# Seven block products for three of the eight branch-gate groups in a hybrid decoder trunk

## The chip, the core and the metric

One NeuronCore of one Trainium2 chip runs the whole trunk. The metric is device time in microseconds (us), the median of several runs. TensorE (PE) has matmuls and weight loads, VectorE (DVE) and ScalarE (ACT) do elementwise work, GpSimd (POOL) issues the accumulating DMAs and SyncE (SP) the other DMAs.

## The reference

Two layers on x (512 tokens, 1024 channels), all in float32. In each layer

- h = RMSNorm(x), and h @ w_in gives all mixers' inputs and the gates, 4 x 1024 columns;
- four branches y_i, 512 wide: sparse attention (A), a convolution module with a 31-tap convolution, a LayerNorm and a swish (B), a short gated convolution (C), stick-breaking attention (D);
- merged = sum over i of sigmoid(gate_i(h) + b_gate_i) * (y_i @ w_o_i), and x = x + merged @ w_merge;
- x = x + FFN(RMSNorm(x)), with gate and up products of 2816 columns, a 3-tap convolution on the gate, and a down product.

## The kernel before, in words

Float32 operands go through the array as float32r pairs: `split` (L187, L188) writes hi = a rounded copy (ACT) and lo = source - hi (DVE), and each product is three matmuls, hi*hi, hi*lo and lo*hi, by `mm` (L123). Activations lie with channels on partitions and 512 tokens on the free side. The normed x is `xh`, `xl`, eight tiles of 128 channels.

Weights come in **units** of 512 KB (1024 elements a partition). `plan` lists all units in the order of use; `ahead` (called by `weights` at each unit) keeps three units split, so that the one in use has two behind it, by `split_weights` (hi on ACT at L414, lo on DVE at L415, three buffers of each). `channels` multiplies one call's units: a unit of 256 columns is two column halves c with 12 matmuls each of 512 tokens, and between the halves it calls `amid`. Outputs take two of four PSUM banks `mm`; other work has four banks `at`.

`amid` calls `tick(budget)`, which emits side jobs from three queues against a budget in us; a job that has several stages gets one stage a tick. `need(labels)` emits, at one place, all that is left up to the labels. PE and DVE run their instructions in the order in which the program emits them (`manual_schedule`, L1349, L707); ACT, POOL and SP are ordered by the scheduler while the mixing runs. In the FFN (L1148) ACT is in emitted order too, and `amid` emits what the dictionary `beside` holds for the running unit number (`slot`).

`merge(n, y)` (L1004 on) takes the branches in the order C, A, D, B (n = 0 to 3). For each of four pairs jj it multiplies 256 gate columns (two units, 1024 inputs), takes the sigmoid on ACT (L1013), multiplies 256 columns of the branch's output map w_o (one unit, 512 inputs), and on DVE multiplies by the gate (L1025) and adds to `merged` (L1027; for n = 3, L1029 and a split).

In queue 2 stand the 31 taps of branch B (L893), then `ln_sum`, a pause, `ln_center` (one product with a constant, then DVE and ACT in turn, L916 to L922), a pause, `ln_root` (four one-column products, a square root on ACT at L278, a reciprocal on DVE at L281), `spread` (four transposes on PE at L286, a copy at L288) and the job `ln`: four `ln_out(c)`, each a DVE multiply (L933), a Silu (L934) and a `split`. They are emitted by the ticks of n = 2 with budget B_M2; after n = 2 stands `need("ln")`, and n = 3 runs with budget 0.

The FFN's gate and up products are done already as **seven block products** (Strassen-Winograd): for 256 + 256 columns, tokens in two halves of H = 256 and inputs in two halves of 512, seven products of a 512 x 256 block with a 512 x 256 block in place of eight. `product` issues 24 matmuls of 256 tokens for each. Their weight blocks are sums, made by accumulating DMAs from GpSimd (`load_sum`, `grow`, L393): s = u1 + u2, then + g1 after the product s1, and so on. The operands are `comb`: "b11", "n1", "b21", "b22" in `xh`, `xl` (written by `feed_ffn`, which keeps first half and difference for the first four tiles), and "t3", "n2", "t4" in tiles of `pieces()`, made by `feed_sums` (two scaled copies on ACT at L251, three DVE operations at L253 to L255, two splits). Partial outputs f, v, y, z pass between products by copies and adds (`start_y` L1172, `keep_y` L1176, `start_z` L1187, `up_half` L1190).

Of the kernel before, what the change touches and what calls it, by code (L numbers as in the profile page):

```python
# [27 lines left out]
P = 128  # L31
# [46 lines left out]
def trunk(ctx: ExitStack, tc, x, positions, g_mix, w_in, b_gate, g_qa, g_ka, g_kidx, w_oa,  # L78
# [15 lines left out]
    def s_tile(w=516, dtype=F32):  # L94
        return tmp.tile([P, w], dtype, tag="s", name=nm("s"), bufs=10)
# [14 lines left out]
    def q4_tile():  # L110
        return act.tile([P, 2, T], F32R, tag="q4", name=nm("q4"), bufs=8)
# [46 lines left out]
    def col(name, i):  # L158
        c = place[name] + i
        return par[:, c:c + 1]  # L160
# [63 lines left out]
    def feed_ffn(k, l):  # L224


        g = col("g_ffn", l * KD + k)
        if k == 0:
            pieces()
# [13 lines left out]
        for i, name in enumerate(("b11", "n1") if k < 4 else ("b21", "b22")):  # L243
            comb[name, k % 4] = [a[k][:, i * H:(i + 1) * H] for a in (xh, xl)]
        squared(k)

    def feed_sums(j, l):

        e1, e2, d, d4 = s_tile(), s_tile(), s_tile(), s_tile()
        for e, k in ((e2, j + 4), (e1, j)):  # L250
            nc.scalar.activation(e[:, :T], xT[k], AF.Copy, scale=col("g_ffn", l * KD + k))  # L251
        t3, n2, t4 = d[:, :H], d[:, H:T], d4[:, :H]
# [9 lines left out]
        comb["t4", j] = four  # L262

    def inv_root(acc, n, rows, sums=None, banks=None):

# [41 lines left out]
    def ffn_block(w, l, h, f):  # L307
        return w[l, h * 512:(h + 1) * 512, f * P:(f + 2) * P]
# [12 lines left out]
    def ffn_order():  # L321
# [4 lines left out]
        for n in range(1, last + 1):  # L326
# [11 lines left out]
            else:  # L338
                yield from ((n, "s3"), (m, "g1"), (n, "s4"), (n, "u2"), (m, "s2"), (m, "g2"))

    def plan():
        for l in range(L):
            for c0, w, nk in V_CHUNKS:
                yield from in_units(l, O_AV + c0, w, nk)
            for p in range(2):
                yield from in_units(l, O_GLU + 512 + 256 * p, 256)
                yield from in_units(l, O_GLU + 256 * p, 256)
            for c in range(2):
                yield from in_units(l, O_AQ + 512 * c, 512, 2)
            for p in range(2):  # L350
                for n in (1, 2, 0):
                    yield from in_units(l, O_CC + 512 * n + 256 * p, 256)
            for n, (branch, w_o) in enumerate(MERGES):
                if n == 1:
                    for i in range(4):
                        yield from in_units(l, O_SB + 256 * i, 256)
                    yield from in_units(l, O_SB + 1024, 512, 2)
                for jj in range(4):
                    yield from in_units(l, O_GATE + branch * D + jj * 256, 256)
                    yield w_o[l, :, jj * 256:(jj + 1) * 256], 0, 4, 256  # L360
            for p in range(4):
# [25 lines left out]
    GROWS = {"s1": ("s", "g1"), "g1": ("g1", "u1"), "s2": ("s", "g2")}  # L387

    def part_of(l, n, name):
        return ffn_block(w_ffn_gate if name[0] == "g" else w_ffn_up, l, int(name[1]) - 1, 2 * n)  # L390

    def grow(l, n, to, what):
# [144 lines left out]
    def tokens(units, ops, w, after=None, between=None, banks=None):  # L537
# [5 lines left out]
        for n, (src, k0, nk, _) in enumerate(units):  # L543
# [15 lines left out]
            if between:  # L559
                tick(budget[0])  # L560
        return ps

    xop = list(zip(xh, xl))

# [110 lines left out]
    def mixing(l, first):  # L675
# [323 lines left out]
                split(y[:, 0], y[:, 1], cv[c][:, :T])  # L999
                yc.append(y)  # L1000

        merged = [None] * KD

        def merge(n, y):  # L1004

            branch, w_o = MERGES[n]
            yop = [(a[:, 0], a[:, 1]) for a in y]
            for jj in range(4):
# [8 lines left out]
                if n == 3:  # L1017
                    hi = q4_tile()
                for c in range(2):
                    j = jj * 2 + c  # L1020
                    if n == 0:
                        merged[j] = mf_tile()
                        nc.vector.tensor_tensor(merged[j], g[c], gs[c][:, :T], op=OP.mult)
                        continue
                    nc.vector.tensor_tensor(gs[c][:, :T], g[c], gs[c][:, :T], op=OP.mult)  # L1025
                    if n < 3:
                        nc.vector.tensor_tensor(merged[j], merged[j], gs[c][:, :T], op=OP.add)  # L1027
                        continue
                    nc.vector.tensor_tensor(gs[c][:, :T], merged[j], gs[c][:, :T], op=OP.add)  # L1029
                    lo = act.tile([P, T], F32R, tag="mf", name=nm("mlo"), bufs=8)  # L1030
                    split(hi[:, c], lo, gs[c][:, :T])
                    merged[j] = (hi[:, c], lo)

        budget[0] = B_M0
        merge(0, yc)
# [92 lines left out]
    BLOCK_OF = {"g1": "b11", "s1": "n1", "s2": "n2", "g2": "b21", "s3": "t3", "s4": "b22",  # L1128
                "u2": "t4"}

    def product(l, n, step, bank):

        hi, lo = block_weights(l, n, step)
        for c in range(2):
            dst = bank[:, c * H:(c + 1) * H]
            for k in range(4):
                oh, ol = comb[BLOCK_OF[step], k]
                w = slice(c * P, (c + 1) * P)
                mm(dst, hi[:, k, w], oh, start=step in ("g1", "s1") and c == k == 0, stop=False)
                mm(dst, hi[:, k, w], ol, start=False, stop=False)  # L1140
                mm(dst, lo[:, k, w], oh, start=False, stop=k == 3)
            if c == 0:
                amid()

    def ffn(l, last):
        done.clear()
        order.close()
        order.enter_context(tc.manual_schedule(engines={E.PE, E.DVE, E.Activation}))  # L1148
# [301 lines left out]
```

## Time and profile before

| what | before |
|---|---|
| median of three runs | 1959.0 us (1958.98 to 1959.74) |
| the profiled execution: time, span | 1959.04 us, 1957.3 us |
| PE busy | 1944.5 us, 99% |
| PE weight loads busy | 1681.5 us, 86% |
| DVE busy | 1407.7 us, 72% |
| ACT busy | 926.5 us, 47% |
| DMA | 237.84 MB, mean 122 GB/s |

The two layers take the same course, 967.3 us apart. A row of the chain gives start, length, the engine with what it did, and a count: "PE mm" are matmuls into the banks `mm`, "PE at" into the banks `at`. A row of a timeline gives start, length, engine, line, operation, output<-input and shape, and in brackets the idle time of the engine before it and what ended that. Where matmuls follow one another, each one's length contains its passage through the array; the distance of starts is the length of a whole row divided by its count.

### The profile page before, as it was taken

To read this page: it belongs to the slowest core of one execution; us is meant where nothing else is said; L and a number is where in the kernel's file an instruction comes from. 1 tells how busy PE (TensorE), PEld (TensorE's weight loads), DVE (VectorE), ACT (ScalarE), POOL (GpSimd) and SP (SyncE) were. 2 spreads that over 40 slices of the span, in tenths; PEclk is the share of its full clock that TensorE was granted. 3 is DMA by queue.
4 is the path that set the end of the run, shared out by engine and by line. 5 is a ranking of instruction groups with operands and counts; after the bars stand their busy time and mean duration, and the time that the engine had idled before them with its cause. 6 is when DMAs were issued, how large, how long until landed. Compare 5 with 4: busy or idle time off the path is not lost.

```text
span 1957.3 us, 27555 instructions
## 1 busy us (share of the span) xinstructions
PE 1944.5 (99%) x10691; PEld 1681.5 (86%) x10691; DVE 1407.7 (72%) x2462; ACT 926.5 (47%) x1494; POOL 120.9 (6%) x173
## 2 busy tenths in 40 slices
PE   9999999999999999999999999999999999999998
PEld 7878888888888998989888888888888889999897
DVE  7887789768446783777867878897674477648675
ACT  6436442443634663634553464424445366546253
POOL 0000000000000210201000000000000012112010
PEclk9999999999999999999999999999999999999999
DMA  6333233323532995966343332332345349769562
GB/s 200 106 97 86 68 89 97 96 98 108 150 97 75 194 202 117 202 166 114 122 129 97 86 87 76 87 97 86 105 122 137 96 98 201 183 134 219 128 120 87
DMA packets 219513, 237.84 MB, mean 122 GB/s; under 512 B 7638, under 2 KB 206838, under 8 KB 218358
## 3 DMA queue, kind: packets, MB, share of 16 engines
q1 hardware_dynamic: 172918, 189.93, 31.7%
q0 software_dynamic: 46464, 46.14, 15.7%
q8 instruction: 84, 1.38, 0.3%
q14 instruction: 47, 0.39, 0.1%
HBM read 229.75 MB, written 6.29 MB: 121 GB/s over the span
## 4 chain that ended last, share of the span: by engine, by line
PE 95%; ACT 2%; DVE 1%; DMA 1%; issue 1%; ACTq 0%; SPq 0%; DVEq 0%; POOLq 0%
PE mm L123 79%; PE at L123 14%; DMA b<-in_w_ffn_gate_dram 1%; ACT hi L414 1%; PE at L841 0%; PE at L1085 0%; PE at L806 0%; DVE lo L415 0%; ACT s L251 0%; PE at L1376 0%; DMA x<-in_x_dram 0%; DVE s L1327 0%; PE at L286 0%; ACT L1214 0%; PE at L745 0%
## 5 line engine op out<-in xcount | busy, mean ns | idle before, releaser
L414 ACT ACTIVATE hi<-raw 128x1024 fp32r<-128x1024 f32 (+2 forms) x297 | 310.4, 1048 | 508.2 <-PE mm L123 460.8
L415 DVE TENSOR_TENSOR lo<-raw,hi 128x1024 fp32r<-128x1024 f32 (+3 forms) x295 | 357.6, 1215 | 207.5 <-ACT hi L414 207.0
L123 PE MATMUL mm<-xh,hi 128*128 128x512 f32 (+1 forms) x1184 | 445.2, 376 | 0.0
L123 PE MATMUL mm<-xh,lo 128*128 128x512 f32 (+1 forms) x1184 | 437.5, 369 | 0.0
L123 PE MATMUL mm<-xl,hi 128*128 128x512 f32 (+1 forms) x1184 | 437.1, 369 | 0.0
L123 PE MATMUL mm<-q,hi 128*128 128x512 f32 x1200 | 381.7, 391 | 0.0
L123 PEld LDWEIGHTS mm<-q,hi 128*128 128x128 f32 x1200 | 224.2, 188 | 47.8 <-issue 2.1
L123 PE MATMUL mm<-q,lo 128*128 128x512 f32 x664 | 258.5, 389 | 0.0
L123 PEld LDWEIGHTS mm<-xh,hi 128*128 128x128 f32 x1184 | 223.3, 189 | 40.6 <-issue 2.8
L123 PEld LDWEIGHTS mm<-xl,hi 128*128 128x128 f32 x1184 | 223.4, 189 | 38.0 <-issue 1.0
L123 PEld LDWEIGHTS mm<-xh,lo 128*128 128x128 f32 x1184 | 223.2, 189 | 38.3
L893 DVE SCALAR_TENSOR_TENSOR b<-b,par,b 128x512 f32<-128x512 f32 x240 | 180.3, 751 | 6.9
L123 PEld LDWEIGHTS mm<-q,lo 128*128 128x128 f32 x664 | 124.6, 188 | 26.0
L123 PE MATMUL at<-xh,lo 128*128 128x256 f32 x480 | 135.8, 283 | 0.0
L123 PE MATMUL at<-xl,hi 128*128 128x256 f32 x480 | 135.8, 283 | 0.0
L123 PE MATMUL at<-xh,hi 128*128 128x256 f32 x480 | 135.8, 283 | 0.0
L123 PE MATMUL mm<-m,hi 128*128 128x256 f32 x660 | 127.0, 283 | 0.5 <-DVE m L188 0.5
L415 DVE TENSOR_TENSOR lo<-b,hi 128x1024 fp32r<-128x1024 f32 x66 | 80.8, 1224 | 61.2 <-ACT hi L414 61.2
L123 PE MATMUL mm<-hi,xh 128*128 128x512 f32 (+1 forms) x320 | 120.3, 382 | 0.6 <-ACT hi L414 0.3
L123 PE MATMUL mm<-lo,xh 128*128 128x512 f32 (+1 forms) x320 | 117.9, 374 | 0.0
L123 PE MATMUL mm<-hi,xl 128*128 128x512 f32 (+1 forms) x320 | 117.8, 374 | 0.0
L414 ACT ACTIVATE hi<-b 128x1024 fp32r<-128x1024 f32 x66 | 69.9, 1059 | 94.6 <-PE mm L123 38.0
(271 smaller groups left out, 3023.5 us busy)
## 6 DMA issues: line engine op xcount, KB each, us to landing
raw<-in_w_in_dram SPq DMA_DIRECT2D x152, 512.0 KB, 3.6
b<-in_w_ffn_gate_dram POOLq DMA_DIRECT2D x44, 512.0 KB, 6.6
raw<-in_w_ffn_down_dram SPq DMA_DIRECT2D x43, 512.0 KB, 4.4
gu<-in_w_ffn_gate_dram SPq DMA_DIRECT2D x22, 512.0 KB, 4.7
b<-in_w_ffn_up_dram SPq DMA_DIRECT2D x22, 512.0 KB, 5.3
b<-in_w_ffn_up_dram POOLq DMA_DIRECT2D x22, 512.0 KB, 6.0
raw<-in_w_ffn_gate_dram SPq DMA_DIRECT2D x22, 512.0 KB
raw<-in_w_ffn_up_dram SPq DMA_DIRECT2D x22, 512.0 KB, 3.7
```

Source lines behind the costliest of these rows:

```text
L123: return nc.tensor.matmul(*a, skip_group_check=True, **k)
L414: nc.scalar.activation(hi[:, k:k + step], raw[:, k:k + step], AF.Copy)
L415: nc.vector.tensor_tensor(lo, raw, hi.bitcast(F32), op=OP.subtract)
L893: nc.vector.scalar_tensor_tensor(a[:, :T], u[c][:, j:j + T], col(f"cb_w{l}", j * 4 + c), a[:, :T], op0=OP.mult, op1=OP.add)
```

## The change

For n = 2 (branch D) the pairs jj = 2, 3 and for n = 3 (branch B) all four pairs are no longer multiplied plainly (`plain_pairs`). Each two pairs, 512 gate columns, are a group done by `gates(n, half, yop)`: seven `product` calls, with the two w_o units of the group at places 0 and 3 of nine. Six groups in two layers are changed; the w_o products, sigmoids, multiplies and adds are the same in number of elements. From the first group on ACT is in emitted order too, and `amid` emits from `beside`, no ticks.

The operands for the groups are made of the normed x: `whole(k)` adds xh and xl; four jobs `sums{j}` after `ln` in queue 2 make "t3", "n2", "t4"; `difference(j)` turns the second half of the first four tiles into a difference. They are wanted at n = 2, jj = 1, between the gate product and the w_o product, with `need("ln", sums0 to sums3)` and four `difference`. `pieces()` is called before n = 2 instead of in `feed_ffn`. The FFN makes its own operands as before.

```diff
+    def whole(k):
+        e = s_tile()
+        nc.vector.tensor_tensor(e[:, :T], xh[k].bitcast(F32), xl[k].bitcast(F32), op=OP.add)
+        return e
+
+    def difference(j):
+        e, d = whole(j), s_tile()
+        nc.vector.tensor_tensor(d[:, :H], e[:, :H], e[:, H:T], op=OP.subtract)
+        split(xh[j][:, H:], xl[j][:, H:], d[:, :H])
...
+    GATE_ORDER = (0, "s1", "g1", 1, "s2", "g2", "s3", "s4", "u2")
+    def plain_pairs(n):
+        return (4, 4, 2, 0)[n]
...
-            for jj in range(4):
+            for jj in range(plain_pairs(n)):
                 g = channels(in_units(l, O_GATE + branch * D + jj * 256, 256), xop, 256)
...
+                if n == 2 and jj == 1:
+                    need("ln", *[f"sums{j}" for j in range(4)])
+                    for j in range(4):
+                        difference(j)
                 g = channels([(w_o[l, :, jj * 256:(jj + 1) * 256], 0, 4, 256)], yop, 256)
+                add_branch(n, jj, g, gs)
+            for half in range(plain_pairs(n) // 2, 2):
+                if slot[0] is None:
+                    slot[0] = 0
+                    order.close()
+                    order.enter_context(tc.manual_schedule(engines={E.PE, E.DVE, E.Activation}))
+                gates(n, half, yop)
...
+            def start_y():
+                v["y"] = ps_at()
+                if first_gates[0]:
+                    v["z"] = ps_at()
+                    for name in "yz":
+                        mm(v[name], identb, zero_diag, start=True, stop=True)
+                nc.scalar.activation(v["y"], v["f"], AF.Copy)
...
+            put(3, start_y)
+            put(5, lambda: keep_y("y2"))
+            put(6, start_z, lambda: sigmoids("f", 0, 0, 1.0))
+            put(7, lambda: keep_y("y3"))
+            put(8, up_half, lambda: sigmoids("z", 0, 1, 1.0), lambda: sigmoids("y3", 2, 1, -1.0),
+                lambda: add_branch(n, 2 * half, v[0], gs[:2]))
+            put(9, lambda: sigmoids("y", 2, 0, -1.0),
+                lambda: add_branch(n, 2 * half + 1, v[1], gs[2:]))
+            for step in GATE_ORDER:
+                if isinstance(step, int):
+                    c = (2 * half + step) * 256
+                    v[step] = channels([(w_o[l, :, c:c + 256], 0, 4, 256)], yop, 256)
+                    continue
+                name = {"g1": "f", "g2": "f", "s1": "v", "s4": "z"}.get(step, "y")
+                if step in ("g1", "s1"):
+                    v[name] = ps_at()
+                product(l, (branch, half), step, v[name])
...
         done.add("room")
+        pieces()
+        for j in range(4):
+            job(2, f"sums{j}", ["ln"], (5.4, lambda j=j: sums(j, whole(j), whole(j + 4))))
         budget[0] = B_M2
+        first_gates[0] = True
         merge(2, yd)
-        need("ln")
-        budget[0] = 0.0
         merge(3, yb)
```

## Rows read from the trace of the kernel before

**Rows 1.** The page, part 1 (busy time of the engines) and part 2 (PE in 40 slices)

```profile
PE 1944.5 (99%) x10691; PEld 1681.5 (86%) x10691; DVE 1407.7 (72%) x2462; ACT 926.5 (47%) x1494; POOL 120.9 (6%) x173
...
PE   9999999999999999999999999999999999999998
```

**Rows 2.** Waits of PE, whole span, longest first: us in total, times, longest

```profile
PE at L123 <- DVE s L1190: 1.7, 1, 1.7
PE mm L123 <- ACT s L1176: 1.3, 2, 0.6
```

**Rows 3.** Chain of waits, 400 to 720 us

```profile
440.30 38.09 PE mm L123 x168
478.39 0.86 PE at L123 x2
479.25 10.92 PE mm L123 x48
490.18 0.79 PE at L123 x8
490.96 5.59 PE mm L123 x24
496.56 0.44 PE at L286 x4
...
687.33 5.76 PE at L123 x48
```

**Rows 4.** Timeline of DVE, first layer, n = 2 and the feeding of the FFN

```profile
467.77 0.74 DVE L893 SCALAR_TENSOR_TENSOR b<-b,par,b 128x512 f32<-128x512 f32 x1
...
486.52 1.22 DVE L415 TENSOR_TENSOR lo<-raw,hi 128x1024 fp32r<-128x1024 f32 x1
...
491.30 0.18 DVE L281 RECIPROCAL rt<-rt 128x4 f32<-128x4 f32 x1 [1.66 <-ACT rt L278]
491.39 0.66 DVE L1025 TENSOR_TENSOR s<-mm,s 128x512 f32<-128x512 f32 x1
...
497.66 0.69 DVE L933 TENSOR_TENSOR b<-b,s 128x512 f32<-128x512 f32 x1 [1.23 <-ACT s L288]
501.26 0.69 DVE L188 TENSOR_TENSOR q<-b,q 128x512 fp32r<-128x512 f32 x1 [2.91 <-ACT q L187]
...
518.72 0.68 DVE L933 TENSOR_TENSOR b<-b,s 128x512 f32<-128x512 f32 x1
524.20 0.69 DVE L188 TENSOR_TENSOR q<-b,q 128x512 fp32r<-128x512 f32 x1 [4.79 <-ACT q L187]
...
631.30 0.43 DVE L253 TENSOR_TENSOR s<-s,s 128x256 f32<-128x256 f32 x1 [0.51 <-ACT s L251]
...
633.50 0.42 DVE L188 TENSOR_TENSOR m<-s,m 128x256 fp32r<-128x256 f32 x1
```

**Rows 5.** Timeline of ACT, first layer, n = 2

```profile
487.32 1.06 ACT L414 ACTIVATE hi<-raw 128x1024 fp32r<-128x1024 f32 x1 [0.86 <-ACT s L1013]
488.28 0.67 ACT L1013 ACTIVATE s<-mm,par 128x512 f32<-128x512 f32 x1
488.97 1.28 ACT L278 ACT_TABLE_LOAD   x1
491.00 0.26 ACT L278 ACTIVATE rt<-at,eps 128x4 f32<-128x4 f32 x1 [0.75 <-PE at L123]
...
497.03 0.60 ACT L288 ACTIVATE s<-at 128x512 f32<-128x512 f32 x1 [2.27 <-PE at L286]
...
498.94 0.82 ACT L934 ACTIVATE b<-b,par 128x512 f32<-128x512 f32 x1
...
500.61 0.61 ACT L187 ACTIVATE q<-b 128x512 fp32r<-128x512 f32 x1
```

**Rows 6.** Timeline of PE, the first microseconds

```profile
1.19 3.17 PE L123 MATMUL at<-s 128*128 128x512 bf16 x7 [1.19 <-DVE s L1364]
...
13.77 2.01 PE L123 MATMUL mm<-hi,xl 128*128 128x324 f32 x12
```

**Rows 7.** Engines by stretch; then DMA issues: KB each, us to landing

```profile
640.00:690.00 50.00, 49.13 (x409) 48.72 (x408) 38.17 (x59) 33.73 (x45) 11.69 (x10) 1.00 1.02 206
...
b<-in_w_ffn_gate_dram POOLq DMA_DIRECT2D x44, 512.0 KB, 6.6
```

More of the change, by code (lines that the diff above doesn't have):

```diff
@@ L247, in feed_sums, with sums @@
     def feed_sums(j, l):
-        e1, e2, d, d4 = s_tile(), s_tile(), s_tile(), s_tile()
+        e1, e2 = s_tile(), s_tile()
         for e, k in ((e2, j + 4), (e1, j)):
             nc.scalar.activation(e[:, :T], xT[k], AF.Copy, scale=col("g_ffn", l * KD + k))
+        sums(j, e1, e2)
+    def sums(j, e1, e2):
+        d, d4 = s_tile(), s_tile()
         t3, n2, t4 = d[:, :H], d[:, H:T], d4[:, :H]
@@ L357, in plan @@
                     yield from in_units(l, O_SB + 1024, 512, 2)
-                for jj in range(4):
+                for jj in range(plain_pairs(n)):
                     yield from in_units(l, O_GATE + branch * D + jj * 256, 256)
                     yield w_o[l, :, jj * 256:(jj + 1) * 256], 0, 4, 256
+                for half in range(plain_pairs(n) // 2, 2):
+                    for step in GATE_ORDER:
+                        if isinstance(step, str):
+                            yield l, (branch, half), step
+                        else:
+                            c = (2 * half + step) * 256
+                            yield w_o[l, :, c:c + 256], 0, 4, 256
             for p in range(4):
@@ L561, in tokens, with product @@
         return ps
+    BLOCK_OF = {"g1": "b11", "s1": "n1", "s2": "n2", "g2": "b21", "s3": "t3", "s4": "b22",
+                "u2": "t4"}
+    def product(l, n, step, bank):
+        hi, lo = block_weights(l, n, step)
+        for c in range(2):
+            dst = bank[:, c * H:(c + 1) * H]
+            for k in range(4):
+                oh, ol = comb[BLOCK_OF[step], k]
+                w = slice(c * P, (c + 1) * P)
+                mm(dst, hi[:, k, w], oh, start=step in ("g1", "s1") and c == k == 0, stop=False)
+                mm(dst, hi[:, k, w], ol, start=False, stop=False)
+                mm(dst, lo[:, k, w], oh, start=False, stop=k == 3)
+            if c == 0:
+                amid()
     xop = list(zip(xh, xl))
@@ L1000, in mixing @@
                 yc.append(y)
-        merged = [None] * KD
+        merged, first_gates = [None] * KD, [True]
         def merge(n, y):
@@ L1007, in merge @@
             yop = [(a[:, 0], a[:, 1]) for a in y]
-            for jj in range(4):
+            for jj in range(plain_pairs(n)):
                 g = channels(in_units(l, O_GATE + branch * D + jj * 256, 256), xop, 256)
@@ new lines, in merge, with add_branch @@
+            for half in range(plain_pairs(n) // 2, 2):
+                if slot[0] is None:
[3 more added lines that the diff above has]
+                gates(n, half, yop)
+        def add_branch(n, jj, g, gs):
+            if n == 3:
+                hi = q4_tile()
+            for c in range(2):
+                j = jj * 2 + c
+                if n == 0:
+                    merged[j] = mf_tile()
+                    nc.vector.tensor_tensor(merged[j], g[c], gs[c][:, :T], op=OP.mult)
+                    continue
+                nc.vector.tensor_tensor(gs[c][:, :T], g[c], gs[c][:, :T], op=OP.mult)
+                if n < 3:
+                    nc.vector.tensor_tensor(merged[j], merged[j], gs[c][:, :T], op=OP.add)
+                    continue
+                nc.vector.tensor_tensor(gs[c][:, :T], merged[j], gs[c][:, :T], op=OP.add)
+                lo = act.tile([P, T], F32R, tag="mf", name=nm("mlo"), bufs=8)
+                split(hi[:, c], lo, gs[c][:, :T])
+                merged[j] = (hi[:, c], lo)
@@ new lines, in gates, with put, keep_y, start_z @@
+        def gates(n, half, yop):
+            branch, w_o = MERGES[n]
+            v, i = {}, slot[0]
+            gs = [None] * 4
+            def put(k, *fs):
+                beside.setdefault(i + k, []).extend(fs)
+            def start_y():
[5 more added lines that the diff above has]
+                nc.scalar.activation(v["y"], v["f"], AF.Copy)
+            def keep_y(name):
+                v[name] = s_tile()
+                nc.scalar.activation(v[name][:, :T], v["y"], AF.Copy)
+            def start_z():
+                if not first_gates[0]:
+                    v["z"] = ps_at()
+                first_gates[0] = False
+                nc.vector.tensor_tensor(v["z"], v["v"], v["y2"][:, :T], op=OP.add)
+            def up_half():
+                nc.vector.tensor_tensor(v["y3"][:, :T], v["v"], v["y3"][:, :T], op=OP.add)
+            def sigmoids(src, tiles, h, sign):
+                for c in range(2):
+                    t = tiles + c
+                    if gs[t] is None:
+                        gs[t] = s_tile()
+                    nc.scalar.activation(
+                        gs[t][:, h * H:(h + 1) * H], v[src][:, c * H:(c + 1) * H], AF.Sigmoid,
+                        bias=col("b_gate", l * 32 + branch * 8 + half * 4 + t), scale=sign)
+            put(3, start_y)
[6 more added lines that the diff above has]
+                lambda: add_branch(n, 2 * half + 1, v[1], gs[2:]))
+            for step in GATE_ORDER:
+                if isinstance(step, int):
+                    c = (2 * half + step) * 256
+                    v[step] = channels([(w_o[l, :, c:c + 256], 0, 4, 256)], yop, 256)
+                    continue
+                name = {"g1": "f", "g2": "f", "s1": "v", "s4": "z"}.get(step, "y")
+                if step in ("g1", "s1"):
+                    v[name] = ps_at()
+                product(l, (branch, half), step, v[name])
@@ L1125, in mixing @@
                     feed_sums(2 * p + c - 4, l)
[L1128 to L1143, printed above, removed]
+        assert not beside
+        slot[0] = None
     def ffn(l, last):
         done.clear()
-        order.close()
-        order.enter_context(tc.manual_schedule(engines={E.PE, E.DVE, E.Activation}))
         rows = act.tile([P, T], F32, tag="rows", name=nm("rows"), bufs=1)
```

23 lines of the change are left out of this document (6 added, 17 removed).

## Prediction, made before the change was run

> **What bounds the kernel now.** I read the page first: PE is busy 99% of the span, in every one of 40 slices [rows 1]. Busy alone could hide small waits, so I read PE's waits next: the longest is 1.7 us in one place, the next 1.3 us in two [rows 2]. TensorE is a full queue from end to end. So a matmul taken out gives back its whole distance to the next one, and any new wait of PE costs its whole length: there is no slack to swallow it. The third view, the chain, gives the distances: 168 matmuls of 512 tokens in 38.09 us are 0.2267 us each, 48 of 256 tokens in 5.76 us are 0.1200 us each [rows 3]. Half the tokens cost 53%, not 50%.
>
> **What is removed and added on PE.** A group of 512 gate columns is two pairs of two units: 4 x 24 = 96 matmuls of 512 tokens, 96 x 0.2267 = 21.77 us. As seven products it is 7 x 24 = 168 matmuls of 256 tokens, 168 x 0.1200 = 20.16 us. A group saves 1.61 us, six save 9.6 us, 4.8 a layer. Against it stand two zero products a layer (the first `start_y`): 512 columns each, by the nearest row 0.23 us, so 0.5 us a layer. This is all that the change can win: 1959.0 - 9.6 + 0.9 = 1950.
>
> The Trainium skill ("TensorE: Matmul & The Clock Gate", "Back-to-back issue gap") gives N/2.4 + 2.5 ns between matmuls; by that a group would save 2.4 us and six some 14 us, an estimate from that page. Here the trace disagrees, with 226.7 and 120.0 ns against 215.8 and 109.2, and I keep the rows.
>
> **What is moved: LayerNorm, sums and differences before the first group.** This is the largest term. In n = 2 of the kernel before, DVE's timeline lets each tick be found: the last tap at 467.77, the LayerNorm's mean, the reciprocal of `ln_root` at 491.30, `ln_out(0)` at 497.66, and `ln_out(3)` from 518.72 to 524.89 [rows 4]. Each tick stands at the middle of a unit. The chain shows them from PE's side: the one-column products of `ln_root` at 490.18 [rows 3] are in the middle of the w_o unit of jj = 1. The new `need` stands half a unit earlier, at 490.18 - 12 x 0.2267 = 487.5. At that point the last pause is over, but `ln_root`, `spread`, four `ln_out`, four `sums` and four `difference` are all still to come, with no unit of matmuls between them.
>
> What PE still has: with three units split ahead, the w_o unit of jj = 1 and the first w_o unit of the group, 48 x 0.2267 = 10.9 us. Behind them comes the product s1. It wants "n1", which the `difference` calls make, and the split of its weights, which `ahead` emits after the burst. DVE keeps the emitted order: at 491.30 it stood 1.66 us idle for a root although the split and adds behind it wanted nothing of it [rows 4]. So s1 waits for the whole burst.
>
> The burst, in the first layer's clock. PE does the one-column products until 488.2. The root waits on ACT for its table, which ends at 488.97 + 1.28 = 490.25, then takes 0.26 [rows 5]; with the reciprocal (0.18) `spread` can start at 490.8. PE is in order too and stands 2.6 us. It goes on at 491.3 (0.44 of transposes) and reaches s1 at 491.3 + 10.9 = 502.2. DVE meanwhile:
> - the copy of `spread`, 0.60, until 491.9 [rows 5];
> - `ln_out(0)`: as before 497.66 to 501.95, with a table load, 4.3 us [rows 4], until 496.2;
> - `ln_out(1 to 3)`: multiply 0.69, Silu 0.82, copy 0.61, lo 0.69 one after the other, with hand-overs 2.9 us each [rows 4, 5], until 504.9;
> - four `sums`: `feed_sums` takes 2.62 us of DVE from 631.30 to 633.92 and each `whole` 0.66 more [rows 4], 3.94 us each, until 520.7;
> - four `difference`: 0.66 + 0.43 + a copy of at most 0.61 + 0.42, some 2.0 us each, until 528.7;
> - lo of s1, 1.22 us [rows 4], until 529.9.
>
> PE waits 529.9 - 502.2 = 27.7 us, with `spread` 30.3 us a layer. From below: if no ACT step held DVE, its instructions alone are 8 x 0.69 + 4 x (1.32 + 3 x 0.43 + 0.69 + 0.42) + 4 x 1.51 + 1.22 = 27.6 us from 487.7 on, until 515.3, against PE at 499.6: 16 us. From above: were each `ln_out` as long as the last one before, 6.2 us, it would be 42 us. I take 30, since with the sigmoids of later gates gone there is one Silu table load where before there were four. Behind DVE's burst stand the adds of jj = 1 and the split of g1, 2.7 + 1.2 us after s1's; s1's own matmuls cover most of that.
>
> **The clock after such a wait.** PE's first matmuls take 3.17 / 7 = 0.45 us for 512 columns, twice the 0.2267 of later, so the lower level, 1.2 GHz; at 13.77 twelve of 324 columns take 2.01 us, 0.17 each, the upper one [rows 6]. No long idle stretch lies inside the trace, so what 27 us of idleness do is bounded: nothing, or half of the 12.6 us from 1.19 to 13.77, 6.3 us. PE was starting and stopping in that stretch and would run densely here; I take 2 us a layer. (The same page, "What's actually happening", holds the throttled level to be what an idle array falls back to; no run here shows it yet.)
>
> **Inside the groups.** Between g2 and s3, s4, u2 no other unit stands. `start_z` comes at the middle of s3 on DVE behind a split (1.22) that waits for a hi (1.06): g2's end + 1.06 + 1.22 + 0.69 = 2.97 against s4 at + 2.88: 0.1 to 0.3 us. The unit after u2 wants the banks of the first w_o unit, free after `up_half` and a multiply: 1.06 + 1.22 + 0.69 + 0.69 = 3.7 us after u2's start, against 2.88: 0.8 us. After the layer's last group the second merge unit needs the last two tiles of `merged`, whose sigmoids, multiplies, adds and splits are emitted only at the middle of the first merge unit; by the same durations DVE and ACT end some 4 us late. From above that is 3 x 1.1 + 4 = 7 us a layer; from below nothing, as the FFN hands partial sums on in the same way at a PE without waits [rows 2, 3]. The gates have less between their steps than the FFN, so I take 4. Weights: a group loads ten units' worth in some 31 us; the FFN's start moves more (DMA share 1.02, PE 49.13 of 50 us [rows 7]), so I put nothing for it. `pieces()` earlier only takes free tiles: nothing.
>
> **Sum.** A layer: - 4.8 + 0.5 + 30.3 + 2 + 4 = + 32; two layers + 64. The profiled execution took 1959.04 us, the median is 1959.0, so the sum stands against either: 2023 us.
>
> **Rivals.**
> 1. *Faster: DVE gets there in time.* The place is the lo of s1: if the burst ends by 502.2, the matmul count decides and the time is 1950. For it: DVE is only 72% busy over the span [rows 1]. Against: even DVE's bare instructions end at 515.3. Chance 0.05.
> 2. *The burst is covered, but the hand-overs in the groups are not*: 1950 + 2 x 7 = 1964. It needs the same condition. Chance 0.04.
> 3. *The burst, and weights that come late besides.* After the wait each group goes through accumulating loads of 6.6 us from issue to landing [rows 7], and s2 needs one that starts when s1 is split. Some 5 us for each of six groups on top: 2050. For it: the DMA share near 1 with such blocks [rows 7]; against: PE stayed dense there. Chance 0.09.
> 4. *The forecast*, chance 0.82.
>
> **Range and chances.** With the lower bound of the burst and nothing for clock and groups, it is 1959 + 2 x (- 4.3 + 16) = 1982; with all the upper bounds, 1959 + 2 x (- 4.3 + 42 + 6.3 + 7) = 2061. All ends meeting is unlikely; 1990 to 2046 leaves out rivals 1 and 2 and about half of what lies at the far ends. A difference below 0.2%, 4 us, is what a measurement of this kernel could not tell from none; of the cases only rival 2 comes near it. Faster 0.05, same 0.02, slower 0.93.
>
> **What would show it.** In the changed profile: two idle stretches of PE of 20 to 35 us, one a layer, ended by DVE's lo of a "b" block or its operand, ahead of the first 256-token products of the mixing; in front of them on DVE L933, the new `whole`, `sums`, `difference`, without a matmul unit between. The products' distance should be 0.1200, and 1008 more matmuls of 256 tokens stand for 576 of 512. The forecast is wrong if PE has no wait above 10 us, or if DVE's burst begins before the end of the gate of jj = 1.

## The result and the profile after

The changed kernel takes 2058.7 us (median of five runs, 2057.6 to 2059.8) against 1959.0 us: a ratio of 1.0508, interval 1.0497 to 1.0519. It is slower by 99.7 us, 49.9 us a layer. The forecast was + 32 a layer, 2023 us, and its range ended at 2046: the direction was right and the time lies outside.

The page of the changed kernel, parts 1 and 2, to be laid beside [rows 1]:

```profile
PE 1958.2 (95%) x11127; PEld 1706.0 (83%) x11127; DVE 1477.4 (72%) x2572; ACT 951.8 (46%) x1566; POOL 151.7 (7%) x197
...
PE   9999999997699899999999999999958998999998
...
PEclk9999999999799999999999999999979999999999
```

PE now has two holes, one a layer, at slices 10 and 11 and at 30 and 31, and a shallower one a layer at slices 14 and 34. In the third row the granted clock, at its upper level throughout in the kernel before, falls at slices 11 and 30. Its mean over the span is 0.978 (1.000 before), so with two levels some 45 us of each layer lie at 1.2 GHz (0.022 x 2 x 2055.8 / 2).

Waits of PE in the changed kernel, longest first (us in total, times, longest), beside [rows 2]:

```profile
PE at L124 <- ACT xh L188: 40.4, 2, 20.2
PE at L124 <- DVE lo L451: 13.8, 4, 6.5
PE at L124 <- ACT hi L450: 10.4, 2, 5.2
PE mm L124 <- ACT q L188: 5.3, 4, 1.3
PE at L305 <- DVE rt L300: 5.3, 2, 2.6
PE mm L124 <- DVE s L1092: 3.7, 6, 0.6
```

Every one comes two or more times, as the two layers take the same course. The timeline of PE in the first layer places the first two rows, ahead of the first product and inside it:

```profile
503.56 0.39 PE L124 MATMUL mm<-q,lo 128*128 128x512 f32 x1
524.16 0.58 PE L124 MATMUL at<-xh,hi 128*128 128x256 f32 x1 [20.21 <-ACT xh L188]
524.62 0.58 PE L124 MATMUL at<-xl,hi 128*128 128x256 f32 x1
531.65 0.58 PE L124 MATMUL at<-xh,lo 128*128 128x256 f32 x1 [6.46 <-DVE lo L451]
```

After two matmuls on the first tile of "n1" PE needs the lo of the weights. The timeline of DVE shows why that is last (the burst; compare [rows 4]):

```profile
490.80 0.18 DVE L300 RECIPROCAL rt<-rt 128x4 f32<-128x4 f32 x1 [2.83 <-ACT rt L297]
492.88 0.69 DVE L986 TENSOR_TENSOR b<-b,s 128x512 f32<-128x512 f32 x1 [1.90 <-ACT s L307]
...
506.46 0.69 DVE L189 TENSOR_TENSOR q<-b,q 128x512 fp32r<-128x512 f32 x1 [1.54 <-ACT q L188]
507.07 1.28 DVE L271 TENSOR_TENSOR s<-xh,xl 128x512 f32<-128x512 f32 x2
...
522.51 0.68 DVE L271 TENSOR_TENSOR s<-xh,xl 128x512 f32<-128x512 f32 x1
...
530.38 1.22 DVE L451 TENSOR_TENSOR lo<-b,hi 128x1024 fp32r<-128x1024 f32 x1
531.52 0.68 DVE L1092 TENSOR_TENSOR s<-mm,s 128x512 f32<-128x512 f32 x1
```

Four `ln_out` from 492.9 to 507.1, four `sums` to 522.5, four `difference` to 530.4, then the lo: one after the other.

A second place was not in the forecast: the FFN's third product (s1 and g1 run before it is fed) starts 61.4 us after the merge's first matmul, against 49.3 in the kernel before. The first matmuls of the merge and of that product, in the kernel before and then in the changed one:

```profile
592.06 0.39 PE L123 MATMUL mm<-q,hi 128*128 128x512 f32 x1
641.33 0.28 PE L123 MATMUL at<-xh,hi 128*128 128x256 f32 x1
```

```profile
626.97 0.50 PE L124 MATMUL mm<-q,hi 128*128 128x512 f32 x1 [0.62 <-DVE s L1092]
688.38 0.58 PE L124 MATMUL at<-xh,hi 128*128 128x256 f32 x1 [5.19 <-ACT hi L450]
```

The clock's share and new waits make the difference. First ACT, then two rows of DVE in the changed kernel ahead of that product:

```profile
687.28 1.04 ACT L450 ACTIVATE hi<-b 128x1024 fp32r<-128x1024 f32 x1
```

```profile
686.44 0.43 DVE L259 SCALAR_TENSOR_TENSOR s<-s,s 128x256 f32<-128x256 f32 x1
...
688.36 1.22 DVE L451 TENSOR_TENSOR lo<-b,hi 128x1024 fp32r<-128x1024 f32 x1 [0.23 <-ACT hi L450]
```

The product's weights are split behind the last `feed_sums` (L259). In the kernel before, DVE's timeline has the same split ahead of the last feeding:

```profile
637.30 1.22 DVE L415 TENSOR_TENSOR lo<-b,hi 128x1024 fp32r<-128x1024 f32 x1
638.44 0.74 DVE L241 SCALAR_TENSOR_TENSOR xl<-h,par,xh 128x512 fp32r<-128x512 f32 x1
```

Engines by stretch in the changed kernel (the fraction behind POOL is the granted clock):

```profile
490.20:493.60 3.40, 2.47 (x8) 2.21 (x9) 0.87 (x2) 1.89 (x4) 0.00 (x0) 0.53 0.28 99
507.20:524.20 17.00, 0.04 (x1) 0.04 (x1) 15.05 (x31) 4.16 (x9) 1.28 (x1) 0.51 0.53 93
524.20:534.60 10.40, 3.94 (x16) 3.48 (x17) 8.85 (x16) 1.25 (x3) 2.26 (x2) 0.50 0.08 7
637.00:643.80 6.80, 5.58 (x12) 4.09 (x13) 2.96 (x4) 2.08 (x3) 0.00 (x0) 0.51 0.24 77
...
683.00:688.10 5.10, 0.19 (x2) 0.00 (x0) 4.02 (x9) 3.82 (x7) 0.00 (x0) 1.00 0.59 94
688.10:695.00 6.90, 6.16 (x27) 5.87 (x28) 3.53 (x4) 3.08 (x5) 2.56 (x2) 0.52 0.43 85
```

Four stretches of a layer, each with or behind a wait, stand at 1.2 GHz, and part of each is dense work: 12 matmuls of 512 tokens take 5.58 us in the fourth row, where 12 x 0.2267 [rows 3] is 2.72.

**The loss of one layer, added up**, in us:

| what | working | us |
|---|---|---|
| savings on PE | as forecast | - 4.3 |
| waits for `spread`, n1 and the lo of s1 | 2.6 + 20.2 + 6.5 | 29.3 |
| hand-overs in the groups | from the end of g1 (538.64) to the merge (626.97) 88.3; matmuls 82.4 | 5.9 |
| lower clock | 1.2 at 490, 2 in s1, 5.58 - 2.72 = 2.9 in the merge, 2.4 in the FFN (22 matmuls in 5.06 us for 2.64) | 8.5 |
| start of the FFN | 5.2 for the hi, 13.8 / 2 - 6.5 = 0.4 for the lo | 5.6 |
| merge: operands that come late | 61.4 - 49.3 - 2.9 - 5.2 | 4.0 |
| sum | | 49.0 |

The 82.4 us of matmuls are 3 x (20.16 + 10.88) = 93.1 for three groups, less s1, g1 and the first w_o unit (11.2), and 0.5 of zeros. Of the 5.9 us left PE is idle for 3.7; the other 2.2 are not assigned to a cause. By the spans the loss is 98.5 / 2 = 49.3 a layer.

### The profile page after: what moved, and what is told of

Same layout as the page of the kernel before. It is cut to its first block, busy times and chain, and to the rows that moved or that the text cites. A ratio compares the mean times of both kernels' runs of the same rounds, so it can differ in the third digit from the quotient of the medians.

```text
span 2055.8 us, 28725 instructions
## 1 busy us (share of the span) xinstructions
PE 1958.2 (95%) x11127; PEld 1706.0 (83%) x11127; DVE 1477.4 (72%) x2572; ACT 951.8 (46%) x1566; POOL 151.7 (7%) x197
## 4 chain that ended last, share of the span: by engine, by line
PE 86%; DVE 5%; ACT 4%; DMA 2%; issue 2%; SPq 0%; POOL 0%; ACTq 0%; DVEq 0%; POOLq 0%
PE mm L124 66%; PE at L124 18%; ACT hi L450 1%; DVE lo L451 1%; DMA b<-in_w_in_dram 1%; DMA raw<-in_w_in_dram 1%; DVE s L1096 1%; ACT q L188 1%; DVE s L1092 1%; PE at L894 0%; PE at L1209 0%; ACT s L250 0%; DVE s L271 0%; PE at L859 0%; DVE mlo L189 0%
## 5 line engine op out<-in xcount | busy, mean ns | idle before, releaser
L451 DVE TENSOR_TENSOR lo<-raw,hi 128x1024 fp32r<-128x1024 f32 (+1 forms) x283 | 343.0, 1214 | 169.2 <-ACT hi L450 168.6
L124 PE MATMUL mm<-xh,hi 128*128 128x512 f32 (+1 forms) x992 | 370.5, 373 | 0.0
L124 PE MATMUL mm<-xh,lo 128*128 128x512 f32 (+1 forms) x992 | 362.9, 366 | 0.0
L124 PE MATMUL mm<-xl,hi 128*128 128x512 f32 (+1 forms) x992 | 362.5, 365 | 0.0
L124 PE MATMUL at<-xh,hi 128*128 128x256 f32 x672 | 194.3, 289 | 50.9 <-ACT xh L188 40.4
L124 PE MATMUL at<-xh,lo 128*128 128x256 f32 x672 | 193.7, 288 | 13.8 <-DVE lo L451 13.8
L124 PE MATMUL at<-xl,hi 128*128 128x256 f32 x672 | 193.3, 288 | 0.0
L124 PEld LDWEIGHTS at<-xh,hi 128*128 128x128 f32 x672 | 132.1, 197 | 52.9 <-ACT xh L188 41.3
L124 PEld LDWEIGHTS at<-xh,lo 128*128 128x128 f32 x672 | 131.7, 196 | 15.0 <-DVE lo L451 15.0
L124 PEld LDWEIGHTS at<-xl,hi 128*128 128x128 f32 x672 | 132.1, 197 | 0.5 <-DVE xl L189 0.3
```

The source lines that it names most:

```text
L124: return nc.tensor.matmul(*a, skip_group_check=True, **k)
L451: nc.vector.tensor_tensor(lo, raw, hi.bitcast(F32), op=OP.subtract)
```

## The experiments

Theory A is that account: separate costs in series, the burst, a clock that falls with each wait, the hand-overs and one unbroken order at the FFN. Its rivals (B) say that the loss lies elsewhere or that a wait taken away only moves on. All diffs are against the changed kernel unless said otherwise.

**One boundary of the emitted order.** The emitted order is closed and opened anew at the FFN's start, as the kernel before did it.

```diff
     def ffn(l, last):
         done.clear()
+        order.close()
+        order.enter_context(tc.manual_schedule(engines={E.PE, E.DVE, E.Activation}))
```

> The change, with the list of engines in emitted order closed and opened again at the start of the FFN, as the kernel before did; nothing else differs. Theory A (the wait ahead of the FFN's third product, 5.5 us a layer plus 0.65, and the slow clock of some 7 us behind it, come from the FFN's weight splits being held behind the last feeding of x on ACT and DVE, in one unbroken emitted order): that wait goes, 9 us a layer, so about 2041 us. Rival B (that wait is for the accumulating load of the FFN's weights, which now starts late): no change beyond 2 us, 2057 to 2060.

Measured 2048.6 us (2045.6 to 2051.6), ratio 1.0456 (1.0419 to 1.0492); its span is 2043.8, 12.0 below the changed kernel's. Waits of PE in this run, the top ones:

```profile
PE at L124 <- ACT xh L188: 40.4, 2, 20.2
PE at L124 <- DVE lo L451: 12.9, 2, 6.5
PE at L305 <- DVE rt L300: 5.3, 2, 2.6
```

The row of 10.4 us for ACT's hi is gone. In its place stand 2.9 us in both layers of short waits for the operand m, which the changed kernel's list does not have. So 5 us a layer (by the medians) to 6 (by the spans) belong to the FFN's start. A had said 2041, so less came back than it said; B had no change.

**The same order in the kernel before.** The diff is against the kernel before, all gates plain: ACT enters the emitted order before branch B and nothing is opened anew at the FFN.

```diff
         budget[0] = 0.0
+        order.close()
+        order.enter_context(tc.manual_schedule(engines={E.PE, E.DVE, E.Activation}))
         merge(3, yb)
...
-        order.close()
-        order.enter_context(tc.manual_schedule(engines={E.PE, E.DVE, E.Activation}))
```

> The kernel before, all gates plain, with one thing of the change: ACT goes into the emitted order at branch B, and the order is not opened anew at the FFN. Theory A (the FFN's start waits in the changed kernel because of that order and not because of the block products): a wait of TensorE of some 5 us ahead of the FFN's third product, a lowered clock behind it, 6 to 9 us a layer, 1971 to 1978 us. Rival B (that wait comes from the late accumulating loads of the changed kernel): 1957 to 1962 us.

Measured 1974.6 us (1973.7 to 1975.3), 1.0076 (1.0060 to 1.0093). Its longest wait of PE, and two stretches, over that wait and behind it:

```profile
PE at L123 <- ACT hi L414: 10.4, 2, 5.2
```

```profile
641.90:648.70 6.80, 1.13 (x6) 0.63 (x4) 5.49 (x11) 5.39 (x9) 0.00 (x0) 0.66 0.44 69
648.70:654.00 5.30, 5.30 (x25) 5.30 (x26) 2.19 (x2) 1.47 (x3) 2.56 (x2) 0.50 0.58 122
```

A's range was met. This settles the FFN's part: without any of the seven products in the mixing the order alone makes the very same wait and 15.3 us, 7.7 a layer: 5.2 of this wait, the rest mostly at the lower clock, which holds over dense work (5.30 of 5.30 us) after the wait has ended.

**No sums, no differences.** The operands of the groups are left out: the products read halves of the normed x in their place, with the same matmuls.

```diff
                 if n == 2 and jj == 1:
                     need("ln", *[f"sums{j}" for j in range(4)])
-                    for j in range(4):
-                        difference(j)
...
-            job(2, f"sums{j}", ["ln"], (5.4, lambda j=j: sums(j, whole(j), whole(j + 4))))
+            job(2, f"sums{j}", ["ln"], (5.4, lambda j=j: stand_in(j)))
```

> The change without the sums and differences of x ahead of the first group: the block products read halves of x itself, so the gates of the three groups are other numbers, and 23.8 us of DVE work a layer are left out. Theory A (the first product waits for DVE's burst): the wait of 20.4 + 6.8 us shrinks to the LayerNorm's part, some 4.7 us, so 24 us a layer less with the clock, about 2010 us. Rival B (the first product waits for its weights, made by accumulating loads): the wait stays over 20 us, 2050 to 2060.

Measured 2019.2 us (2018.7 to 2019.8), 1.0305 (1.0276 to 1.0335). The making of operands costs 39.5 us of the 99.7, the largest part, but 9 us less than A had it. Waits of PE:

```profile
PE at L124 <- ACT hi L459: 10.4, 2, 5.2
PE at L124 <- DVE lo L460: 9.2, 4, 4.2
PE at L124 <- ACT s L1127: 6.3, 3, 3.0
```

What is left at the first product is the LayerNorm's part of the burst (lo, 4.2), and a wait for a copy of `keep_y`, 6.3 us in all, that was 0.9 in the changed kernel. So part of a removed wait comes back behind it.

**Two groups in place of three.** The burst comes a pair later, at jj = 3, and branch D stays plain.

```diff
-        return (4, 4, 2, 0)[n]
+        return (4, 4, 4, 0)[n]
...
-                if n == 2 and jj == 1:
+                if n == 2 and jj == 3:
```

> Two groups a layer in place of three: branch D is multiplied plainly, only branch B by block products, and the operands are wanted at the last pair of branch D, so that the LayerNorm and one job of sums are emitted by the ticks with units of matmuls between them. Theory A (wait = DVE burst less the 10.9 us of matmuls that cover it): the burst is three sums, four differences and a split, 21 us; the wait is some 10 us and its clock 2 us; with 2.7 us saved and the tail and the FFN's start as they are, 27 us a layer, about 2013 us. Rival B (the block products' weights hold them up at the first group): the wait stays above 20 us, 2035 us or more.

Measured 2026.3 us (2026.3 to 2026.4), 1.0342 (1.0312 to 1.0372); A said about 2013. Waits of PE at the first product:

```profile
PE at L124 <- ACT xh L188: 15.7, 2, 7.9
PE at L124 <- DVE lo L451: 13.8, 4, 6.5
```

14.4 us a layer, where A had counted on about 10. A had counted three sums in the burst, but all four stand in it: the gate product of jj = 3 issues its last matmul at 520.9, and DVE begins the first sum behind that.

```profile
521.29 1.29 DVE L271 TENSOR_TENSOR s<-xh,xl 128x512 f32<-128x512 f32 x2
```

The two units of w_o end at 532.3 and cover two of the sums and part of the third; the rest of the sums, the differences and the lo have no cover. The wait depends on how much is still to come at `need`, as A says; its size was taken too low again.

**Matmuls ahead of the first product, to keep PE at work.** Zero products of 512 columns are issued before s1: 92 in the changed kernel, 126 with the boundary of the first experiment.

```diff
+                if step == "s1" and first_gates[0]:
+                    pad = ps_at()
+                    for _ in range(92):
+                        mm(pad, identb, zero_diag, start=True, stop=True)
```

> The change with 92 matmuls of zeros on 512 columns (some 20 us) put on TensorE in the place where it waits for the first product's operands; their output is not used. The wait itself is as long. Theory A (the idle time costs twice, once as wait and once as a lower clock for the products behind it): the products after the wait run at the upper clock, 1.5 to 3 us a layer less, 2053 to 2056 us. Rival B (the clock behind the wait costs nothing): 2058 to 2060; a time above that means that the zeros outlast the wait.

> The run with the order opened anew at the FFN, and 126 matmuls of zeros on 512 columns (some 28 us) in the place where TensorE waits ahead of the first product, so that it is idle neither before the product nor between its first matmuls. Theory A (idle time lowers the clock for what comes behind it, 1.5 to 3 us a layer there): no lowered clock from 500 to 540 us in the trace, s1 and g1 at 0.12 us a matmul, 3 to 6 us less than the run with the order alone, 2043 to 2046 us against its 2048.6. Rival B: the same time within 1.5 us or more.

With 92: 2056.8 us (2054.8 to 2058.8), 1.0497 (1.0467 to 1.0528), between the two expectations. The padding ended at 524.7, PE did two matmuls and then stood 6.7 us for the lo, the granted clock was 0.51 from 530.3 to 537.2, and nothing follows from it. With 126: 2045.9 us (2044.4 to 2047.4), 1.0438 (1.0416 to 1.0461), its two stretches from the padding on:

```profile
503.60:531.60 28.00, 28.00 (x132) 12.86 (x130) 22.58 (x44) 8.26 (x16) 2.57 (x2) 1.00 0.36 71
531.60:537.40 5.80, 5.53 (x47) 5.37 (x46) 5.04 (x7) 0.00 (x0) 2.56 (x2) 1.00 0.64 90
```

Now s1 and g1 run at 2.4 GHz, 47 matmuls in 5.53 us, where the changed kernel had 0.21 us for one. So the clock falls because PE stands, not because of these products. Its price there, some 4 us in two layers, is within the spread of the runs of the first experiment (2045.6 to 2051.6): the trace shows the effect, the time does not settle its size.

**The burst spread out.** Two sums go into the pauses ahead of the LayerNorm, two behind the first products, the differences stay at the last pair before the groups; the last group's two w_o units are moved towards its end so that the merge's operands come earlier, and the boundary stands at the FFN. Once with two groups, once with three (then one sum ahead, three behind).

```diff
+        for j in range(2):
+            job(2, f"sums{j}", ["room"], (3.9, lambda j=j: sums(j, whole(j), whole(j + 4))))
...
-                if n == 2 and jj == 1:
-                    need("ln", *[f"sums{j}" for j in range(4)])
+                if n == 2 and jj == 3:
+                    need("ln", *[f"sums{j}" for j in range(2)])
...
+    LAST_ORDER = ("s1", "g1", 0, "s2", "g2", "s3", "s4", "u2", 1)
...
+            for j, k in ((2, 1), (3, 2)):
+                if kept:
+                    put(k, lambda j=j: sums(j, kept.pop(j), whole(j + 4)))
```

> Two groups a layer, with no burst: two of the four sums are side jobs in LayerNorm's pauses, at the last pair of branch D only the four differences (8 us) and the split stand ahead of the first product, against 10.9 us of matmuls, and the other two sums come at places 1 and 2 of the first group, ahead of the product that wants them. The last group ends with its w_o unit, so that sigmoids and adds of the gates have cover; the FFN's start opens the emitted order anew. Theory A (burst without cover, uncovered tail, one unbroken order are all of the loss; the products themselves gain 1.6 us a group): no wait of TensorE above 2 us in the gates and at the FFN's start, 1959.4 - 5.5 = 1954 us, up to 1957 with 0.9 us hand-overs in a group. Rival B (block products in the mixing lose time of themselves, by weights or hand-overs, whatever the operands): 1963 us or more.

> Three groups a layer with the same order of work as in the run with two groups: one sum in LayerNorm's pause, three sums at places 0 to 2 of the first group, the last group ending with its w_o unit, the emitted order opened anew at the FFN. Root, spread, four LayerNorm outputs and four differences still stand with no unit between them ahead of the first group. Theory A: DVE needs some 3 + 16.5 + 8 + 1.2 us there against 10.9 us, so 2.6 + 13 us of wait and 3 us of clock a layer; with 4.4 saved 14 us a layer are lost, about 1988 us. Rival B (the order of sums is not what holds the first product): the wait stays at 27 us, 2015 or more.

Two groups: 2000.2 us (1999.0 to 2002.0), 1.0207 (1.0190 to 1.0224). Three groups: 2026.3 us (2025.5 to 2027.2), 1.0340 (1.0320 to 1.0361). Both missed A's number by far, and their times are on B's side; but the wait of 27 us that B said would stay with three groups did not stay. The waits of PE with three groups:

```profile
PE at L124 <- DVE lo L457: 12.9, 2, 6.5
PE at L124 <- ACT xh L188: 9.5, 2, 4.8
PE at L124 <- ACT at L1129: 9.2, 4, 2.8
PE at L124 <- ACT s L1133: 9.2, 2, 5.2
```

The wait at the first product fell from 26.7 to 11.3 us a layer, and 9.2 came back as waits for `start_y` (L1129) and `keep_y` (L1133): the sums put behind s1 and g1 hold up the copies that the next products want. In neither of the two orders tried does that stretch have room for the work.

**Towards the best version.** Four more kernels, each built on the one before. First: two groups in the change's own order, two sums in the LayerNorm's pauses, the other two at places 1 and 2 of the first group, the multiplies that free the banks put ahead of `up_half`, and the boundary at the FFN.

```diff
+        early = [(0.0, lambda j=j: sums(j, whole(j), whole(j + 4))) for j in range(2)]
+        job(2, "centered", ["room"], (1.8, ln_sum), early[0], (4.8, ln_center), early[1], (0.1, ln_root),
...
+            put(8, lambda: sigmoids("z", 0, 1, 1.0), lambda: times(v[0], gs[:2]), up_half,
```

> Two groups a layer; the two early sums stand in LayerNorm's two pauses, so that its outputs keep their ticks; differences at the last pair of branch D; the other sums at places 1 and 2 of the first group; both groups in the order of the change; in a group the multiplies that free the banks of the first w_o unit come ahead of the other adds; order opened anew at the FFN. Theory A (only uncovered work costs): no wait above 1 us at the first group, where the run before it had 4.8 and 2.1; the tail behind the last group stays, 4.5 us and 3 us of clock a layer; 1959.4 - 5.5 + 15 = 1969 us, 1962 to 1976. Rival B (products in the mixing lose of themselves): 1985 or more.

Measured 1987.8 us (1987.0 to 1990.9), 1.0145 (1.0129 to 1.0161), in B's part. The lo of s1 still costs 3.1 us a layer and the operands of the merge come late. Second, against the first: the merge's first two outputs share their first halves, so that the late tiles of `merged` are wanted a unit later.

```diff
+        for p in range(2):
+            merge_half(p, 0)
         for p in range(4):
-            ps = channels(merge_units(l, p), merged, 256)
+            if p < 2:
+                merge_half(p, 1)
+                ps = first[p]
```

> The same, and behind the last group the first two output pairs of the merge product share their first halves: units of inputs 0 to 511 for both, then those of inputs 512 to 1023, so that the last gates' adds have 10.9 us of matmuls in place of 5.4. Theory A (the tail is the chain of multiply, add and split for the last two tiles, 4 us too long for one unit): the waits behind the last group fall below 1 us and the clock stays up, 6 to 7 us a layer less than the run beside it, 1954 to 1960 us. Rival B (the tail is something else): no change against it.

Measured 1983.5 us (1982.4 to 1984.1), 1.0118 (1.0100 to 1.0136): 4 us less, but at the merge a wait of 1.8 us for a multiply of the last group stays, and the expectation was 1954 to 1960 for A and no change for B. Third, against the second: three units split before the differences, and ACT out of the emitted order while the merge runs.

```diff
                     need("ln")
+                    ahead(3)
...
+        order.close()
+        order.enter_context(tc.manual_schedule(engines={E.PE, E.DVE}))
         first = [[ps_mm() for _ in range(2)] for _ in range(2)]
```

> The run with two groups and shared merge halves, with two more edits: the weights of the first product are split ahead of the differences, and ACT leaves the emitted order for the merge product, as in the kernel before. Theory A (each wait left is a place in the emitted order): the wait of 3.3 us inside the first product and the 2.1 us at the FFN's start go, with 2 to 5 us of clock a layer, some 9 us a layer, about 1965 us; what is then left above the 2.8 us saved is the hand-overs inside the groups, 5 to 6 us a layer, so it does not come below the kernel before. Rival B (the waits move to the next place instead): 1978 or more.

Measured 1976.0 us (1975.5 to 1977.0), 1.0086 (1.0071 to 1.0101), between A's 1965 and B's 1978. With the lo early, PE waits for each piece of "n1" in its place:

```profile
PE at L124 <- ACT xh L188: 5.2, 6, 1.0
```

Fourth, against the third: no burst at all. The differences get a tile of their own, so they need not wait for the last reader of xh, and each is made inside `ln_out` between ACT's copy and DVE's lo; the second half of x is loaded back only after branch B, and the two last sums are jobs again; the early splits of the third kernel are left out.

```diff
-        split(xh[j][:, H:], xl[j][:, H:], d[:, :H])
+        split(own["t"][:, j, 0], own["t"][:, j, 1], d[:, :H])
...
-            split(y[:, 0], y[:, 1], a)
+            nc.scalar.activation(y[:, 0], a, AF.Copy)
+            difference(c)
+            nc.vector.tensor_tensor(y[:, 1], a, y[:, 0].bitcast(F32), op=OP.subtract)
```

> Two groups a layer as in the last of the two-group runs, with the differences in tiles of their own (room is made by loading the second half of x again only after branch B), so that they need not wait for the last plain gate: each stands inside one LayerNorm output, where DVE waits for ACT anyway, and the last two sums follow by ticks. Nothing stands in a burst any more. Theory A (the burst was the cost of the first group): no wait above 1 us at the first product, 7 us a layer less and some clock, 1958 to 1963 us; below 1959.3 only if the hand-overs inside the groups shrink too. Rival B (a first product after plain units waits whatever is done ahead of it): above 1968.

Measured 1968.5 us (1967.2 to 1970.4), 1.0048 (1.0034 to 1.0061). The edge between the theories was 1963 and 1968, so this is B by half a us. Engines by stretch in the first layer, from ahead of the first product to the FFN's third:

```profile
533.10:538.90 5.80, 5.80 (x50) 5.78 (x49) 4.00 (x6) 2.05 (x2) 0.00 (x0) 1.00 1.24 198
538.90:593.30 54.40, 52.85 (x365) 48.29 (x363) 29.39 (x33) 25.55 (x39) 7.69 (x6) 1.00 0.78 185
593.30:642.70 49.40, 49.40 (x241) 41.90 (x242) 39.40 (x63) 30.11 (x48) 3.88 (x3) 1.00 0.38 99
```

The first product is dense, the clock is 1.00 throughout, the way from the merge to the FFN is 49.4 us, where it was 49.3. Two groups save 2.7 us a layer, yet the FFN's third product starts 1.4 us later than before (642.69 against 641.33), so 4.1 us went into hand-overs and small waits: some 3 of them inside the two groups, and 0.9 ahead of them, 0.7 of it a wait for a sigmoid at the start of the first w_o unit. The second layer holds more (a wait of 2.8 us for a copy of the LayerNorm, 3.4 us at 0.50 from 1502.6 on), which were not tried one by one. None of these kernels is faster than the kernel before. A's times were met twice, by the one order in the kernel before and by the long padding; in every other run less came back than A said.

## Why the prediction was right and wrong

The forecast of + 32 a layer fell 18 short. The burst, its largest term, held. Three steps failed: the clock was put at 2 and measured some 8.5, the hand-overs were put at 4 and measured 9.9, and the start of the FFN, 5.6 of waiting, had no term.

**Matmuls: right.** 1008 more of 256 tokens stand for 576 of 512; with the four zero products that is 436 more, and the count is 11127 for 10691. Two products in the chain of the changed kernel:

```profile
565.79 5.75 PE at L124 x48
```

5.75 / 48 = 0.1198 us, as in the row with 0.1200. The rule of the Trainium skill ("TensorE: Matmul & The Clock Gate", "Back-to-back issue gap") that the prediction set aside gives an estimate of 0.1092; this trace disagrees with it too.

**The burst: right in mechanism, place and size.** Forecast `spread` 2.6 and s1 27.7; measured 2.6 and 26.7. Some luck is in how closely it agrees: PE was done with the units in front at 503.95, not 502.2, and the lo ended at 531.6, not 529.9, so both ends came 1.7 later. The parts too: LayerNorm's end 504.9 forecast and 507.1 measured, sums 3.94 each and 3.87, differences 2.0 and 1.97, the lo's end 529.9 and 531.6. That DVE is 72% busy over the span [rows 1] said nothing; adding up one engine's queue between two points of PE's did. Rivals 1 and 2 fell with it.

**"The clock after such a wait ... I take 2 us a layer": mis-sized.** It measured some 8.5, above the bound of 6.3. The forecast looked for one wait and one recovery. There were four, since with the waits at 490, at the merge and at the FFN the clock fell as well, and each cost 1.2 to 2.9 us in matmuls at up to twice their distance. The forecast's bounds came from the first 12.6 us of the kernel before, read by the distance of matmuls alone: the granted clock of that stretch is 1.00, so its rows do not record a lower level there. The Trainium skill ("TensorE: Matmul & The Clock Gate", "What's actually happening") holds the throttled level to be what an idle array falls back to. This trace agrees, with 0.51 from 507.2 to 524.2 while PE stood. In the stretch of the FFN's wait, 683.0 to 688.1, the granted clock was still 1.00, though, and 0.52 behind it, when PE was at work again.

**"Inside the groups ... I take 4": mis-sized.** The groups took 5.9 and the merge 4.0, 9.9 together, more than the 7 of the upper bound. The single steps were near: the unit after u2 waits 0.6 for its banks (0.8 forecast), the merge's operands come 4.0 us late (4 forecast). But the groups lose 2.0 us each where two steps gave 1.1, and I had taken about half of what the steps gave, because the FFN hands over in the same way without waits [rows 2, 3]; that likeness did not hold.

**"From the first group on ACT is in emitted order too": read and not costed.** The prediction has no term for it; by the trace it cost 5.6 of waiting and 2.4 of clock a layer, and the first two experiments show it from both sides with 5 to 6 and 7.7 us a layer. In the kernel before, the boundary at the FFN left the split of the third product's weights ahead of the last feeding; the unbroken order put it behind.

**Range.** The upper end of 2046 was set by asking how unlikely it is that all bounds meet. But they are not independent: the four places of a layer with larger waits came with slow stretches, so the terms rise together (the hand-overs in the groups, at most 0.7 us each, left the granted clock at 1.00 from 544.6 to 626.9). Rival 3, late weights, does not show: no wait above is ended by a transfer of weights. It comes near in one place: the chain of the second layer leads through an accumulating load to a hi, and from there to a wait of PE of 0.25 us at 1567.89.

```profile
1557.77 8.41 DMA b<-in_w_in_dram
```

**What stays open.** The first layer is accounted for to within 1 us, the second by its equal waits only. The clock's share was isolated in the trace but not in time, the hand-overs inside the groups are a difference of times and were not tested by a run of their own, and the further waits of the second layer in the last experiment were not separated.

## What to carry to other kernels

Where PE is full, price a change by adding up each in-order queue between the point at which its work may start and the point at which PE wants it; an average of busy time hides a burst of 40 us. If a form of product saves 1.6 us and needs five hand-overs, ask first whether each of them has other matmuls beside it. And where an edit extends or moves a region of emitted order, compare the order on every engine at the region's old boundaries, for that can cost more than the edit itself wins.

## What was unexpected of the hardware

The granted clock fell with short waits too: 0.53 from 490.2 to 493.6, where PE had done eight one-column products and then stood 2.6 us for `spread`, and 0.51 from 637.0 to 643.8, among the merge's small gaps. After the long wait the lower level stayed until about 534.6, while PE had been dense since 531.65. Some of these kernels also vary more from run to run: the two runs of the first experiment took 2045.6 and 2051.6 us, with a mean granted clock of 0.982 and 0.978. The run with two groups did not (2026.3 and 2026.4), so what sets the spread is open.
